# A two-layer hybrid decoder on one core: rests of the attention, pooling and gate weights by a negative copy and an adding transfer, with new priorities

## The chip, the core and the metric

The kernel runs on one core of a Trainium2 chip. The core has a matrix engine (TensorE, PE in the profile; its weight loads are PEld), VectorE (DVE), ScalarE (ACT), GpSimd (POOL) and SyncE (SP), which here only issues transfers. The engines run at the same time, each takes its instructions in order, and they wait for one another through semaphores. The metric is the device time of one execution in microseconds; less is better.

## What is computed

Two layers over 512 tokens of width 1024, then a last norm. Each layer has a sparse attention in which every query attends to its 128 best keys by an indexer's score, a gated linear attention, a pooling over trailing windows, and a convolutional feed-forward part. All in float32.

```python
def hybrid_layer(x, ...):
    h = rms_norm(x, norm1_g)
    qa, ka, va, qi, ki, wi, qb, kb, vb, rb, gl, uc = split_cols(h @ w_in)
    o_a = dsa_attention(rope(qa), rope(ka), va, rope(qi), rope(ki), wi)   # top-k keys, then softmax
    o_b = rms_norm(gla_chunked(qb, kb, vb, log_a(gl))) * silu(rb)
    o_c = multiscale_pool(uc, w_pool, pool_scale)
    x = x + concat(o_a, o_b, o_c) @ w_out
    return x + conv_glu_ffn(rms_norm(x, norm2_g), w_up, conv_w, conv_b, w_down)
```

## The kernel before

**Exact products of rounded halves.** The matrix engine takes float32 operands in a rounded format (F32R). So each operand is split into a rounded half and a rest, and `mm3` makes three matmuls of each product: rounded by rounded, rounded by rest, rest by rounded. For activations `split` and `split_scaled` do this. For weights `weights` (L567 on) does it. It cuts a matrix into chunks; of each chunk SyncE loads `raw` from memory (three buffers, `NRAW`), ACT copies it into the rounded half `hi`, and DVE subtracts the two into the rest `lo` (five buffers each, `NW`). A chunk of w_rb, w_uc, w_qk, w_gqk, w_qi, w_out and w_up is 128 partitions by 1024 values, as is one of w_v; those of w_tok and w_down are mostly smaller. `chunk` multiplies a 256-column matrix with the activations (output by columns), `tokens` makes the output by tokens (w_tok, 340 columns, and w_v, 512).

**The stages of a layer.** `layer` writes the work down in parts, by `nc.part`: start, qi, tok, ki (indexer), score1 to 3 and top1 to 3 (scores and the choice of keys of three query blocks, `choose`, sixteen rounds of maximum and replacement on DVE each), rb, gqk and gla (gates and the gated linear attention, whose chain runs over GpSimd, ACT and DVE), v, uc (pooling), qk (four chunks pairs of queries and keys; `rope` turns them with copies on SyncE's queue, `stacked` and `paired` lay their halves out with more copies), att0 to 3 (attention of each query block), out and ffn. In the times of the profile layer 0 lies at 0 to 632 us, its attention stage ending about 221; layer 1 follows, its attention stage ending about 821.

**What sets the order.** Nothing is issued as it is written. `Plan.take` records each instruction with a cost (`price`), its tiles and its dependences; `depend` adds an edge between two that touch the same data, with a delay for the signal from engine to engine (`delay`). `schedule` then orders all by a list plan in four passes: `forward` starts, on each engine that is free, the ready instruction of the highest priority for which buffers are free, and `backward` gives the priorities of the next pass. `HASTE` adds hand-set nanoseconds to the priority of a part, a part in a layer, or a part in a layer on an engine. A tile's buffer counts as free again some time after its last user ended: 2000 ns for SyncE's transfers, 200 ns for all others. `emit` issues the instructions of all engines in the order of the planned starts. On the chip each engine keeps that order, and only the semaphores decide when it goes on. Nearly all rows of the profile thus bear one line, L519, that of `emit`, and are told apart by their tiles.

The three lines at the heart of `weights`:

```python
nc.sync.dma_start(out=raw, in_=src[:, k0 * n:(k0 + kn) * n])
nc.scalar.activation(out=hf.bitcast(F32R), in_=raw, func=AF.Copy)
nc.vector.tensor_tensor(out=lf.bitcast(F32R), in0=raw, in1=hf, op=OP.subtract)
```

`price` has a branch for a transfer issued by GpSimd already (1050 ns); the kernel before has no such transfer.

Of the kernel before, what the change touches and what calls it, by code (L numbers as in the profile page):

```python
# [12 lines left out]
F32R = mybir.dt.float32r  # L13
I32 = mybir.dt.int32
U32 = mybir.dt.uint32
AF = mybir.ActivationFunctionType
OP = mybir.AluOpType
# [4 lines left out]
KC = D // P  # L22
# [30 lines left out]
def _constants():  # L53
# [26 lines left out]
    for c in range(2):  # L80
# [19 lines left out]
HASTE = {"top2": -52700, "gla": 1500, "score1": 43300, "att3": -100, "top3": -239100, "att0": 55600,  # L100
         "top1": -4600, "out": -7000, "rb": -6100, "rope": 68500, "ffn": 6800, "end": -97000, "end1": -7700,
# [31 lines left out]
         "gqk": 900}  # L133
WAVE = 1.2
SWITCH = 95.0
# [11 lines left out]
class Op:  # L147
    __slots__ = ("eng", "cost", "calls", "preds", "succs", "tiles", "func", "tags", "port", "shapes")

    def __init__(self, eng):  # L150
        self.eng, self.cost, self.calls = eng, 0.0, []
        self.preds, self.succs, self.tiles, self.func, self.tags = {}, {}, set(), None, set()
        self.port, self.shapes = False, []
# [12 lines left out]
class Plan:  # L166
# [50 lines left out]
    def depend(self, i, region, write):  # L217
        name = region[0]
        op = self.ops[i]
        old = self.access.setdefault(name, [])  # L220
        keep = []
        for j, r, w in old:
            if j != i and (write or w) and self.overlap(region, r):
                self.edge(j, i, self.delay(self.ops[j].eng, op.eng))
            covered = write and region[1] <= r[1] and r[2] <= region[2] and region[3] <= r[3] and r[4] <= region[4]
            if not covered or j == i:
                keep.append((j, r, w))
        keep.append((i, region, write))
        self.access[name] = keep
        op.tiles.add(name)  # L230

    def take(self, eng, fn, method, args, kw):
        out = kw.get("out", args[0] if args else None)
        ins = [x for k, x in list(enumerate(args)) + list(kw.items()) if hasattr(x, "tensor") and x is not out and k != "accum_out"]
        outs = [out] + ([kw["accum_out"]] if "accum_out" in kw else [])
        if self.open:
            op, i = self.ops[self.open[0]], self.open[0]
        else:
            op, i = Op(eng), len(self.ops)
# [6 lines left out]
        op.port = op.port or self.shared(eng, method, ins, out)  # L246
        if eng == "pe":
            rows, cols = (ins[0].shape[0], out.shape[0]) if method != "transpose" else (P, P)
            shape = tuple(32 if x <= 32 else 64 if x <= 64 else P for x in (rows, cols))
            if not op.shapes or op.shapes[-1] != shape:  # L250
                op.cost += SWITCH * bool(op.shapes)
                op.shapes.append(shape)
# [272 lines left out]
class Kern:  # L525
# [41 lines left out]
    def weights(self, src, k, n, whole=False):  # L567
        nc = self.pl
        out = []
        step = k if whole else min((k + 1) // 2, 1104 // n)  # L570
        for k0 in range(0, k, step):
# [6 lines left out]
            hf = hi.rearrange("p k n -> p (k n)")  # L578
# [3 lines left out]
            nc.vector.tensor_tensor(out=lf.bitcast(F32R), in0=raw, in1=hf, op=OP.subtract)  # L582
# [211 lines left out]
    def tokens(self, src, n):  # L794

        w = self.weights(src, KC, n)
# [347 lines left out]
    def layer(self, l):  # L1144
# [44 lines left out]
        w = self.weights(a["w_rb"][l], KC, 256)  # L1189
# [15 lines left out]
        w = self.weights(a["w_uc"][l], KC, 256)  # L1205
        for m in range(2):
            self.pool(l, m, self.chunk(w, m))
        for c in range(4):
            nc.part = "qk"
            w = self.weights(a["w_qk"][l, c], KC, 256)  # L1210
# [268 lines left out]
```

## Time and profile before

| | us |
|---|---|
| median of 3 runs (1227.28 to 1227.61) | 1227.35 |
| the profiled execution | 1230.25 |
| its span, first to last instruction | 1228.4 |
| PE busy | 1213.7 |
| DVE busy | 692.4 |
| ACT busy | 505.2 |
| GpSimd busy | 327.3 |

The span is what the trace covers; the profiled execution took 1.85 us more around it. A stretch is named by its microseconds from the start of the span. The granted clock is TensorE's, as a share of its full speed: 1.00 is the higher of its two levels, 2.4 GHz, 0.50 the lower, 1.2 GHz. Matmuls are pipelined, so that the busy spans of two of them overlap, and a busy PE need not be at its peak.

### The profile page before, as it was taken

To read this page: it belongs to the slowest core of one execution; us is meant where nothing else is said; L and a number is where in the kernel's file an instruction comes from. 1 tells how busy PE (TensorE), PEld (TensorE's weight loads), DVE (VectorE), ACT (ScalarE), POOL (GpSimd) and SP (SyncE) were. 2 spreads that over 40 slices of the span, in tenths; PEclk is the share of its full clock that TensorE was granted. 3 is DMA by queue.
4 is the path that set the end of the run, shared out by engine and by line. 5 is a ranking of instruction groups with operands and counts; after the bars stand their busy time and mean duration, and the time that the engine had idled before them with its cause. 6 is when DMAs were issued, how large, how long until landed. Compare 5 with 4: busy or idle time off the path is not lost.

```text
span 1228.4 us, 16614 instructions
## 1 busy us (share of the span) xinstructions
PE 1213.7 (99%) x6188; PEld 998.4 (81%) x6188; DVE 692.4 (56%) x1249; ACT 505.2 (41%) x819; POOL 327.3 (27%) x276
## 2 busy tenths in 40 slices
PE   9999999999999999999999999999999999999997
PEld 7878788888888888888897777888888888888887
DVE  7479986454553345444535999646355433454432
ACT  6562368443332134333425414864334322333331
POOL 1464351223221022221205623512122200222211
PEclk9999989999999999999999999999999999999998
DMA  8332464222223322224443135523222233332321
GB/s 272 112 95 76 129 158 138 69 87 85 87 71 105 125 94 99 90 78 126 147 137 92 52 109 153 152 86 103 69 95 89 89 95 114 103 103 92 95 72 69
DMA packets 49888, 129.38 MB, mean 105 GB/s; under 512 B 7488, under 2 KB 10320, under 8 KB 49808
## 3 DMA queue, kind: packets, MB, share of 16 engines
q1 hardware_dynamic: 49376, 128.05, 33.6%
q8 instruction: 49, 0.80, 0.3%
q10 hardware_dynamic: 432, 0.27, 0.1%
q14 instruction: 31, 0.25, 0.1%
HBM read 109.22 MB, written 4.26 MB: 92 GB/s over the span
## 4 chain that ended last, share of the span: by engine, by line
PE 87%; DVE 8%; issue 2%; POOL 2%; ACT 1%; DMA 0%; DVEq 0%; POOLq 0%; ACTq 0%
PE mm L519 78%; PE aux L519 9%; DVE score L519 2%; DVE m L519 2%; DVE lo L519 1%; DVE pl L519 1%; DVE qt L519 0%; POOL sl L519 0%; DVE att L519 0%; DMA raw<-in_w_out 0%; DVE q L519 0%; ACT L519 0%; POOL ke L519 0%; DVE k L519 0%; POOL ex L519 0%
## 5 line engine op out<-in xcount | busy, mean ns | idle before, releaser
L519 PE MATMUL mm<-xh,hi 128*128 128x512 f32 x960 | 379.8, 396 | 1.4 <-DVE q L519 1.2
L519 PE MATMUL mm<-xh,lo 128*128 128x512 f32 x960 | 374.7, 390 | 0.0
L519 PE MATMUL mm<-xl,hi 128*128 128x512 f32 x960 | 374.5, 390 | 0.0
L519 DVE TENSOR_TENSOR lo<-raw,hi 128x1024 fp32r<-128x1024 f32 (+3 forms) x210 | 244.6, 1173 | 181.4 <-ACT hi L519 178.6
L519 ACT ACTIVATE hi<-raw 128x1024 fp32r<-128x1024 f32 (+3 forms) x210 | 203.2, 975 | 341.4 <-PE mm L519 293.4
L519 PEld LDWEIGHTS mm<-xh,hi 128*128 128x128 f32 x960 | 180.6, 188 | 43.5 <-issue 6.6
L519 PEld LDWEIGHTS mm<-xh,lo 128*128 128x128 f32 x960 | 180.6, 188 | 38.4 <-DVE lo L519 0.4
L519 PEld LDWEIGHTS mm<-xl,hi 128*128 128x128 f32 x960 | 180.8, 188 | 36.5 <-issue 0.7
L519 PE MATMUL mm<-h,hi 128*128 128x512 f32 (+1 forms) x470 | 180.1, 383 | 0.0
L519 PE MATMUL mm<-h,lo 128*128 128x512 f32 (+1 forms) x470 | 178.3, 379 | 0.0
L519 PE MATMUL mm<-l,hi 128*128 128x512 f32 (+1 forms) x470 | 178.3, 379 | 0.0
L519 POOL TENSOR_TENSOR cv<-cv,rstd 128x512 f32<-128x512 f32 x44 | 57.9, 1318 | 299.9 <-ACT cv L519 292.0
L519 POOL TENSOR_TENSOR l<-cv,h 128x512 fp32r<-128x512 f32 x44 | 70.0, 1592 | 157.2 <-ACT h L519 149.0
L519 PEld LDWEIGHTS mm<-h,lo 128*128 128x128 f32 x470 | 88.4, 188 | 16.7
L519 PEld LDWEIGHTS mm<-h,hi 128*128 128x128 f32 x470 | 88.4, 188 | 16.5 <-issue 0.5
L519 PEld LDWEIGHTS mm<-l,hi 128*128 128x128 f32 x470 | 88.5, 188 | 15.8
L519 DVE SCALAR_TENSOR_TENSOR cv<-a,vec,cv 128x511 f32<-128x511 f32 (+1 forms) x88 | 71.8, 820 | 32.1 <-ACT cv L519 30.8
L519 ACT ACTIVATE cv<-a,vec 128x512 f32<-128x512 f32 x44 | 35.7, 814 | 125.2 <-DVE a L519 125.2
L519 DVE TENSOR_TENSOR a<-mm,rstd 128x512 f32<-128x512 f32 x44 | 30.3, 692 | 100.5 <-PE mm L519 100.4
L519 DVE TENSOR_TENSOR x<-x,mm 128x512 f32<-128x512 f32 (+1 forms) x50 | 33.1, 665 | 78.7 <-PE mm L519 75.3
L519 POOL TENSOR_TENSOR sq<-sq,sq 128x512 f32<-128x512 f32 x23 | 34.2, 1488 | 141.4 <-ACT sq L519 141.3
L519 ACT ACTIVATE cv<-cv 128x512 f32<-128x512 f32 x44 | 27.6, 632 | 61.2 <-DVE cv L519 61.2
(197 smaller groups left out, 1393.9 us busy)
## 6 DMA issues: line engine op xcount, KB each, us to landing
raw<-in_w_up SPq DMA_DIRECT2D x88, 512.0 KB, 3.8
raw<-in_w_down SPq DMA_DIRECT2D x32, 384.0 KB, 3.1
raw<-in_w_down SPq DMA_DIRECT2D x32, 320.0 KB, 2.9
raw<-in_w_qk SPq DMA_DIRECT2D x16, 512.0 KB, 3.8
raw<-in_w_out SPq DMA_DIRECT2D x16, 512.0 KB, 4.0
x<-in_x SPq DMA_DIRECT2D x16, 256.0 KB, 5.0
raw<-in_w_v SPq DMA_DIRECT2D x8, 512.0 KB, 4.1
raw<-in_w_rb SPq DMA_DIRECT2D x4, 512.0 KB, 4.2
```

The lines of the kernel that those rows point to most:

```text
L519: self.issued(i, fn(*args, **kw))
```

## The change

In `weights` a new argument `adds` selects how the rest is made. Where it is set, ACT makes a second copy, of `hi` times -1 into `lo`, and GpSimd's queue issues a transfer of `raw` into `lo` that adds to what is there. Where it is not set, DVE subtracts as before. It is set for w_rb, w_v (the only one with 512 columns), w_uc and w_qk, in both layers. The unused argument `whole` goes. The planner gets `LANDING`: a transfer issued by GpSimd delays all that depend on it by 3500 ns more. All of `HASTE` is replaced.

```diff
-HASTE = {"top2": -52700, "gla": 1500, "score1": 43300, "att3": -100, "top3": -239100, "att0": 55600,
...
-         "gqk": 900}
+HASTE = {"top2": -24800, "gla": 1500, "score1": 56200, "top3": -308500, "att0": 26200, "top1": -4500,
...
+         "qk.1": 3000, "att1.1.act": -4500, "qk": -100, "qi.1.pe": 300, "tok.0.pe": -400, "rb.0.act": 600}
 WAVE = 1.2
+LANDING = 3500.0
...
-    __slots__ = ("eng", "cost", "calls", "preds", "succs", "tiles", "func", "tags", "port", "shapes")
+    __slots__ = ("eng", "cost", "calls", "preds", "succs", "tiles", "func", "tags", "port", "shapes", "late")
...
-        self.port, self.shapes = False, []
+        self.port, self.shapes, self.late = False, [], 0.0
...
-                self.edge(j, i, self.delay(self.ops[j].eng, op.eng))
+                self.edge(j, i, self.delay(self.ops[j].eng, op.eng) + self.ops[j].late)
...
+        if eng == "pool" and method == "dma_start":
+            op.late = LANDING
...
-    def weights(self, src, k, n, whole=False):
+    def weights(self, src, k, n, adds=False):
...
-        step = k if whole else min((k + 1) // 2, 1104 // n)
+        step = min((k + 1) // 2, 1104 // n)
...
-            nc.vector.tensor_tensor(out=lf.bitcast(F32R), in0=raw, in1=hf, op=OP.subtract)
+            if adds:
+
+                nc.scalar.activation(out=lf.bitcast(F32R), in_=hf, func=AF.Copy, scale=-1.0)
+                nc.gpsimd.dma_start(out=lf, in_=raw, accum_op=OP.add)
+            else:
+                nc.vector.tensor_tensor(out=lf.bitcast(F32R), in0=raw, in1=hf, op=OP.subtract)
...
-        w = self.weights(src, KC, n)
+        w = self.weights(src, KC, n, n == 512)
...
-        w = self.weights(a["w_rb"][l], KC, 256)
+        w = self.weights(a["w_rb"][l], KC, 256, True)
...
-        w = self.weights(a["w_uc"][l], KC, 256)
+        w = self.weights(a["w_uc"][l], KC, 256, True)
...
-            w = self.weights(a["w_qk"][l, c], KC, 256)
+            w = self.weights(a["w_qk"][l, c], KC, 256, True)
```

## Rows read from the trace of the kernel before

**Rows 1.** Page, section 1: busy us (share of the span) and instructions of each engine.

```profile
PE 1213.7 (99%) x6188; PEld 998.4 (81%) x6188; DVE 692.4 (56%) x1249; ACT 505.2 (41%) x819; POOL 327.3 (27%) x276
```

**Rows 2.** Stretches: us, busy us (count) of PE, PEld, DVE, ACT, POOL; clock, DMA share, GB/s.

```profile
80.00:146.00 66.00, 65.79 (x320) 49.60 (x318) 65.62 (x169) 17.35 (x24) 26.59 (x28) 1.00 0.29 93
146.00:164.00 18.00, 17.55 (x153) 13.02 (x152) 17.74 (x44) 10.51 (x19) 7.26 (x6) 1.00 0.72 180
164.00:176.00 12.00, 11.80 (x63) 10.32 (x63) 8.01 (x29) 5.83 (x18) 7.53 (x6) 0.57 0.40 120
176.00:221.00 45.00, 45.00 (x405) 37.54 (x404) 28.19 (x99) 37.86 (x105) 11.47 (x9) 1.00 0.44 125
221.00:632.00 411.00, 411.00 (x1846) 342.20 (x1845) 192.53 (x220) 145.44 (x189) 87.89 (x59) 1.00 0.32 101
...
660.00:720.00 60.00, 58.16 (x294) 45.06 (x293) 55.70 (x134) 24.69 (x40) 32.12 (x41) 1.00 0.26 82
720.00:782.00 62.00, 59.72 (x369) 46.02 (x368) 59.45 (x151) 28.19 (x55) 20.00 (x16) 1.00 0.55 151
782.00:821.00 39.00, 38.68 (x379) 32.23 (x379) 19.05 (x75) 31.21 (x93) 10.63 (x8) 1.00 0.37 113
```

**Rows 3.** Waits of PE: engine waited for, us in total, times, longest us.

```profile
PE mm L519 <- DVE q L519: 1.2, 1, 1.2
PE aux L519 <- POOL ke L519: 1.2, 1, 1.2
...
PE aux L519 <- DVE att L519: 0.5, 1, 0.5
```

**Rows 4.** Timeline of PE, 719 to 722 us: start us, us, what, [idle before <-releaser].

```profile
719.71 0.39 PE L519 MATMUL mm<-xh,lo 128*128 128x512 f32 x1
721.32 0.47 PE L519 MATMUL mm<-xh,hi 128*128 128x512 f32 x1 [1.22 <-DVE q L519]
```

**Rows 5.** DMA issues: out<-in, engine, operation xcount, KB each, median us to landing.

```profile
raw<-in_w_qk SPq DMA_DIRECT2D x16, 512.0 KB, 3.8
...
raw<-in_w_v SPq DMA_DIRECT2D x8, 512.0 KB, 4.1
raw<-in_w_rb SPq DMA_DIRECT2D x4, 512.0 KB, 4.2
raw<-in_w_uc SPq DMA_DIRECT2D x4, 512.0 KB, 4.9
s0h<-sh SPq DMA_DIRECT2D x16, 128.0 KB, 2.4
```

**Rows 6.** Instructions by form: count | busy us, mean ns | idle before; last row 80 to 146 alone.

```profile
L519 DVE TENSOR_TENSOR lo<-raw,hi 128x1024 fp32r<-128x1024 f32 x140 | 178.2, 1277 | 110.5 <-ACT hi L519 107.8 <-PE aux L519 0.8
...
L519 ACT ACTIVATE hi<-raw 128x1024 fp32r<-128x1024 f32 x140 | 148.0, 1060 | 191.8 <-PE mm L519 160.8 <-issue 21.1 <-DMA raw<-in_w_rb 3.3
...
L519 DVE TENSOR_TENSOR lo<-raw,hi 128x1024 fp32r<-128x1024 f32 x11 | 13.3, 1213 | 0.0
```

**Rows 7.** Waits of all engines, columns as in rows 3: the rounding copy on ACT.

```profile
ACT hi L519 <- PE mm L519: 293.4, 128, 7.8
```

**Rows 8.** One issue on SyncE (timeline); one operation on GpSimd (instructions by form).

```profile
150.11 0.55 SPq L519 DMA_DIRECT2D rot<-q  x1
...
L519 POOL TENSOR_TENSOR sl<-q,sa 128x512 fp32r<-128x512 f32 x8 | 10.4, 1294 | 16.6 <-PE mm L519 8.1 <-ACT sa L519 6.1 <-ACT hi L519 2.2
```

**Rows 9.** Timelines of ACT and DVE in layer 1: a rounding copy, and its subtraction.

```profile
705.26 1.06 ACT L519 ACTIVATE hi<-raw 128x1024 fp32r<-128x1024 f32 x1 [3.96 <-PE mm L519]
...
711.26 2.33 DVE L519 TENSOR_TENSOR lo<-raw,hi 128x1024 fp32r<-128x1024 f32 x2
```

**Rows 10.** SyncE's queue: its longest wait; its timeline from 691 us.

```profile
SPq L519 <- DVE lo L519: 828.8, 181, 23.0
...
691.18 28.22 SPq L519 DMA_DIRECT2D raw<-in_w_qk  x5
721.25 0.52 SPq L519 DMA_DIRECT2D rot<-q  x1
```

More of the change, by code (lines that the diff above doesn't have):

```diff
@@ L99 @@
 PASSES = 4
-HASTE = {"top2": -52700, "gla": 1500, "score1": 43300, "att3": -100, "top3": -239100, "att0": 55600,
-         "top1": -4600, "out": -7000, "rb": -6100, "rope": 68500, "ffn": 6800, "end": -97000, "end1": -7700,
[31 rows of a table removed]
-         "gqk": 900}
+HASTE = {"top2": -24800, "gla": 1500, "score1": 56200, "top3": -308500, "att0": 26200, "top1": -4500,
[31 rows of a table added]
 WAVE = 1.2
+LANDING = 3500.0
 SWITCH = 95.0
```

61 rows, old and new, of the table HASTE are left out of this document.

## The prediction

> **What bounds the kernel now.** I read the busy shares first: TensorE (PE) is busy 1213.7 of 1228.4 us, VectorE (DVE) 692.4, ScalarE (ACT) 505.2, GpSimd (POOL) 327.3 [rows 1]. So PE's work is a floor that this change does not touch: it adds and removes no matmul. A gain can only come out of time in which PE waits or runs slowly. The cut into stages says where that is [rows 2]. In the feed-forward stretch 221 to 632 us PE is busy all of 411.00 us: nothing to win. The attention stages are different. In layer 0 PE lacks 0.21 us in 80 to 146, 0.45 in 146 to 164 and 0.20 in 164 to 176, together 0.9 us. In layer 1 it lacks 1.84, 2.28 and 0.32 us in the three stretches from 660 to 821, together 4.4 us. Beside that stands the granted clock: 0.57 on average over 164 to 176, so that PE is at the lower of its two levels (1.2 of 2.4 GHz) for most of it, and loses about (1 - 0.57) x 12 = 5.2 us of full-rate work there. The reader is to see in the same rows that DVE is the full engine: 65.62 of 66 us in 80 to 146, 55.70 of 60 and 59.45 of 62 in layer 1, while ACT is busy only 17.35 of 66 and GpSimd 26.59 of 66.
>
> Then I read who ended PE's waits [rows 3]: the longest is DVE's evacuation of q, 1.2 us, with another 0.5 behind DVE's work on att; GpSimd's ke holds PE for 1.2. The first one in order of time [rows 4]: matmuls follow one another about 0.23 us apart, each is shown 0.39 long, and the one at 719.71 is followed only at 721.32. The view reports 1.22 us of idle time where the gap in starts is 1.61, so it understates a wait by some 0.16 us, and waits shorter than that do not show at all.
>
> **Part 1: 32 subtractions leave DVE.** The pooling, gate and attention weights are the chunks of w_rb (4), w_v (8), w_uc (4) and w_qk (16), 32 in all [rows 5]. Each has one DVE subtraction of 128x1024. Its mean is 1.277 us over the whole run and 1.213 in 80 to 146 [rows 6], so DVE is relieved of 32 x 1.21 = 39 us, 19 per layer. In 80 to 146 us there are eleven of them; the last two are of w_out, whose loads come behind those of w_qk, and stay. So 9 x 1.21 = 11 of the 66 us go, and about as much from the full part of layer 1. This is no 39 us of time: PE is fed meanwhile from other chains. What DVE directly costs PE there is 1.2 + 0.5 = 1.7 us [rows 3]; I take all of it. Of the other 4.4 - 1.7 = 2.7 us of idle time in layer 1, GpSimd's ke among it, which itself comes out of the DVE chain of the gates, I take half, 1.4 us. What is late next is ACT: in 176 to 221 it is already busy 37.86 of 45 [rows 2], and nothing of the change relieves that stretch.
>
> **Part 2: 32 negative copies on ACT.** The nearest row is ACT's own rounding copy of the same shape, 1.060 us [rows 6], so 32 x 1.06 = 34 us, 17 per layer. Those of w_uc and w_qk land in 80 to 146 and 660 to 740, where ACT is idle more than half of the time [rows 2], those of w_rb and w_v ahead of it; that idle time hides them. If that cover is gone, as in 176 to 221, a copy costs its 1.06 us. Behind a copy on ACT's queue wait the next rounding copy and the gate chain's exponentials. The rounding copy usually waits for PE to give back a weight buffer anyway, 293.4 us in 128 waits [rows 7]. I take 0.
>
> **Part 3: 32 transfers on GpSimd's queue.** No row of before shows a transfer issued by GpSimd or one that adds, so both prices are bounded. The issue: below by SyncE's 0.55 us for one transfer, above by GpSimd's 1.294 for an ordinary operation on 128x512 [rows 8]; I take 1.1, nearer the second because it is that engine's own. That is 32 x 1.1 = 35 us on an engine that is 27% busy [rows 1]. The landing: below by the 2.4 us of a 128 KB copy inside the core, above by twice the 3.8 us of a 512 KB load, 7.6, since the sum must also read its destination [rows 5]; I take 5. The Trainium skill (DMA: Bandwidth & Descriptors, section on the anatomy of one DMA on the GpSimd path) fits such a transfer at about 2.0 us plus bytes over 436 GB/s, an estimate of 3.2 us for 512 KB; no run here shows one yet, the loads of that size took 3.8 from SyncE, and with 3.2 in place of 5 the sum below would be the same, as only the cover grows.
>
> A rest is thus ready 1.06 + 1.1 + 5 = 7.2 us (4.0 to 10.0) after its rounding copy, with no DVE queue in between. Today it is 1.2 us at best, but in the full stretch also more: the rounding copy of one w_qk chunk runs at 705.26 to 706.32 and the two subtractions next in line start at 711.26 [rows 9]. Does PE starve? A chunk feeds 24 matmuls x 0.23 = 5.5 us of PE, and five buffers leave four chunks, 22 us, of lead. 10.0 is below 22, so I cost the delay at nothing; that cover would be gone only if GpSimd held the issue back for more than 12 us.
>
> The transfer is a wait added to GpSimd's in-order queue: it waits for ACT's copy, and ke, kt, ex and osq of the gates are queued behind it. One hold of about the issue, 1.1 us, on something that PE waits for already (ke, 1.2 us), is likely in one or the other layer: I charge 1.5 us, with 0 to 4 as bounds. The raw buffer, too, is given back only at the landing: 7.2 - 1.2 = 6 us later than a prompt subtraction would.
>
> **Part 4: the new priorities.** All work is ordered anew, from a plan that now adds 3.5 us for the landing. The order of PE's work between 146 and 176 is what the clock hangs on: the fall at 164 comes behind 18 us in which weight loads were busy 13.02 us (72%) and PE sat between short attention matmuls; in 80 to 146 it was 49.60 of 66 (75%), in 720 to 782 46.02 of 62 (74%), and neither lost its clock [rows 2]. [...] With 11 us less DVE work ahead of this stretch, attention reaches PE earlier, while it still has weight chunks to mix in. I take the fall as gone, 5.2 us; a fall of the same length elsewhere would cost the same, and is the next case.
>
> **The sum.** 1.7 + 1.4 + 5.2 - 1.5 = 6.8 us. The profiled execution took 1230.25 us, 1.85 of it outside its span of 1228.4; it is 2.9 us above the median of the runs, 1227.35. Against itself: 1230.25 - 6.8 = 1223.45; against the median, which is what is asked: 1220.5.
>
> **Rivals.** (a) The low clock stays, or comes elsewhere; the waits go. 1227.35 - 1.6 = 1225.7, between 1223.5 and 1226.5. For it: the short attention matmuls of 146 to 164 stay as they are, and only their order changes. (b) More goes: all idle time of the two stages (0.9 + 4.4), the clock's 5.2 and as much again in waits too short to show: 1227.35 - 10.5 - 5 = 1212. For it: DVE is full for 130 us in both layers; against it: PE's idle time is small. (c) The relief is hidden anyway: PE's other chains end no earlier, and a stall moves from DVE to ACT. 1226.5 to 1228.5. (d) Slower: SyncE's in-order queue. The next load of raw weights waits for the buffer, today for DVE's subtraction (828.8 us in 181 waits), and then for the transfer's landing. Behind the loads on that queue stand the copies that turn and pair q and k: from 691.18 five loads of w_qk fill 28.22 us, and the first rot copy goes at 721.25 [rows 10]. The planner adds the 3.5 us to whoever reads the rest, but in its forward pass gives the raw buffer back 0.2 us after the issue, so its order of SyncE is too early by 3.3 us and more. It decides from the point where PE has used up its weight chunks before the pairs are there, about 146 and 740. Then 3 to 6 us per layer come on top, less the 3.1 of part 1: 1227.35 + 6 to 12 - 3 = 1230 to 1236. Against it: GpSimd's transfers themselves stand on another queue, and by 4 of 5 buffers the loads run early.
>
> **How the numbers follow.** Forecast 0.40 (1215 to 1223), (a) 0.22, (b) 0.10, (c) 0.08, (d) 0.20. About 0.2%, 2.5 us, is what a measurement of this kernel can tell from no change, so faster means under 1224.9: the forecast, (b) and half of (a), 0.61. Within: the other half of (a) and nearly all of (c), 0.18. Slower: (d) and a rest of (c), 0.21. The range leaves about one in ten out at either end: 1212 to 1232, from (b) to the lower half of (d).
>
> **What would show it.** Right: no subtraction rows of w_rb, w_v, w_uc and w_qk on DVE, ACT up by some 34 us, DVE down by some 39; DVE below full in 80 to 146; no wait of PE for DVE's q; the clock at 1.00 between 140 and 180. Landings of 4 to 7 us would confirm part 3. Wrong: PE waits that are ended by a transfer into lo, or SyncE waiting for such landings ahead of the rot copies, then (d); a low clock elsewhere, then (a); PE's idle time unchanged with ACT in DVE's place, then (c).

## The result, and the profile after

The changed kernel is slower. Its median is 1254.28 us (1252.02 to 1255.99, four runs) against 1227.48 us (1227.28 to 1228.71) of the kernel before, run beside it: a ratio of 1.0214 [1.0202, 1.0226]. That is 26.8 us more, where 6.8 less were forecast. The profiled execution took 1252.02 us, its span 1249.9, which is 21.5 us more than the span of before. Nearly all rows of after bear line L520, the one of `emit`.

The busy shares first, in the columns of [rows 1]:

```profile
PE 1214.7 (97%) x6188; PEld 999.0 (80%) x6188; DVE 675.8 (54%) x1217; ACT 533.7 (43%) x849; POOL 344.8 (28%) x308
```

PE's busy time is nearly as it was (1213.7 in [rows 1]), so it stands still for 1249.9 - 1214.7 = 35.2 us instead of 14.7. These 20.5 us of standing are all but one of the 21.5 us that the span grew by. The stretches say where; the columns are those of [rows 2]. The stretch 20 to 80 us of before was not among those rows, so it stands here, ahead of those of after:

```profile
20.00:80.00 60.00, 59.96 (x310) 50.71 (x310) 36.62 (x74) 35.27 (x54) 26.05 (x25) 1.00 0.44 134
```

```profile
20.00:80.00 60.00, 52.80 (x265) 44.25 (x265) 27.17 (x56) 36.50 (x48) 31.73 (x34) 0.94 0.79 202
80.00:146.00 66.00, 64.97 (x346) 49.48 (x345) 59.65 (x166) 29.40 (x43) 24.72 (x32) 1.00 0.50 123
146.00:164.00 18.00, 11.93 (x55) 9.35 (x54) 14.04 (x34) 5.29 (x8) 5.79 (x5) 0.81 0.54 155
164.00:176.00 12.00, 12.00 (x91) 9.53 (x91) 10.15 (x28) 5.43 (x14) 2.83 (x3) 1.00 0.76 180
...
221.00:632.00 411.00, 411.00 (x1894) 340.56 (x1893) 200.21 (x230) 152.13 (x209) 87.60 (x60) 1.00 0.31 98
...
660.00:720.00 60.00, 55.93 (x282) 43.08 (x281) 43.52 (x108) 36.31 (x55) 37.83 (x42) 0.97 0.54 127
720.00:782.00 62.00, 56.03 (x313) 44.00 (x311) 57.69 (x143) 22.65 (x31) 22.26 (x26) 1.00 0.73 178
```

PE lacks 7.2 us in 20 to 80 (0.04 before), 6.1 in 146 to 164 (0.45 before), 4.1 and 6.0 in layer 1 (1.8 and 2.3 before), and nothing in the feed-forward stretch. Read the column of the DMA engines beside it: 0.79 for 0.44, 0.50 for 0.29, 0.54 for 0.26, 0.73 for 0.55. In the feed-forward stretch, which has no new transfer, it is 0.31 for 0.32. Where PE stands and where the share grew do not match stretch by stretch: in 80 to 146 PE lacks only 1.0 us, and in 146 to 164 the share fell (0.54 for 0.72) while PE lacks 6.1. The last column but one of [rows 2] had the numbers of before, and the prediction did not use them.

The parts themselves, in the columns of [rows 6]: the subtractions left, the rounding copies, the negative copies on ACT, and the issues on GpSimd.

```profile
L520 DVE TENSOR_TENSOR lo<-raw,hi 128x1024 fp32r<-128x1024 f32 x108 | 141.2, 1312 | 102.1 <-ACT hi L520 97.2 <-PE aux L520 2.9
...
L520 ACT ACTIVATE hi<-raw 128x1024 fp32r<-128x1024 f32 x140 | 147.7, 1059 | 200.6 <-PE mm L520 186.1 <-DMA raw<-in_w_v 4.1 <-issue 3.2
...
L520 ACT ACTIVATE lo<-hi 128x1024 fp32r<-128x1024 f32 x32 | 33.5, 1053 | 0.6
...
L520 POOL DMA_DIRECT2D lo<-raw x32 | 28.9, 912 | 81.7 <-ACT lo L520 74.7 <-ACT relu L520 3.2 <-DVE small L520 2.0
```

DVE lost 32 subtractions, 178.2 - 141.2 = 37 us of them, though its busy time fell by 16.6 only, as others of its operations were stretched (the 56 products qt from 23.0 to 35.2 us). ACT gained 33.5 us of copies, and a transfer's issue holds GpSimd for 0.91 us. What PE and SyncE wait for, in the columns of [rows 3]:

```profile
PE mm L520 <- DVE q L520: 11.5, 4, 6.1
PE aux L520 <- DVE qt L520: 7.8, 3, 5.1
PE aux L520 <- DMA sa<-sl: 3.4, 1, 3.4
...
PE mm L520 <- DMA lo<-raw: 1.0, 1, 1.0
...
SPq L520 <- DVE lo L520: 722.4, 163, 21.0
SPq L520 <- DMA lo<-raw: 172.9, 29, 21.8
```

PE hardly waits for a rest itself (1.0 us). It waits for DVE's q and qt and for a copy inside the core, sa. The transfers of after, with the columns of [rows 5] and, in the first line, the new queue's packets, megabytes and share of the 16 DMA engines' time:

```profile
q0 software_dynamic: 4608, 16.78, 7.0%
...
lo<-raw POOLq DMA_DIRECT2D x32, 512.0 KB, 5.5
...
sa<-sl SPq DMA_DIRECT2D x12, 128.0 KB, 3.8
...
rot<-q SPq DMA_DIRECT2D x8, 64.0 KB, 4.2
rot<-k SPq DMA_DIRECT2D x8, 64.0 KB, 5.0
```

The same three small copies in the kernel before:

```profile
sa<-sl SPq DMA_DIRECT2D x12, 128.0 KB, 2.3
...
rot<-q SPq DMA_DIRECT2D x8, 64.0 KB, 2.0
rot<-k SPq DMA_DIRECT2D x8, 64.0 KB, 2.0
```

So copies that the change does not touch take 1.7 to 2.5 times as long to land. Two places show how that and GpSimd's queue reach PE. The first is PE's longest single wait, at 150 us. In order of time, the timelines of SyncE, DVE and PE (columns as in [rows 4]):

```profile
139.09 0.69 DVE L520 TENSOR_TENSOR k<-mm,rstd 128x512 f32<-128x512 f32 x1
...
140.58 3.14 SPq L520 DMA_DIRECT2D raw<-in_w_out  x2
143.77 1.56 SPq L520 DMA_DIRECT2D rot<-k  x1
...
149.96 0.01 DVE L520 LOAD_MASK_SELECT sh<-rot  x1 [6.14 <-DMA rot<-k]
...
156.07 0.67 DVE L520 TENSOR_TENSOR q<-mm,rstd 128x512 f32<-128x512 f32 x1
...
156.79 0.79 PE L520 MATMUL mm<-xh,hi 128*128 128x512 f32 x1 [6.07 <-DVE q L520]
```

What SyncE's queue waited for just then, 138 to 143.5 us (columns of [rows 3]):

```profile
SPq L520 <- DMA lo<-raw: 10.9, 2, 8.5
```

k is ready at 139.78, but rot<-k, its 64 KB copy, stands behind two loads of w_out on SyncE's queue, and these wait for the landings of two rests, the first 8.5 us and the second 2.4. So the copy is issued at 143.77, 4.0 us late, and it lands 6.0 us later, where such copies took 2.0 before (median): about half of its delay is the hold of the queue, half the longer landing. DVE, whose next instruction reads it, stands for 6.14 us until 149.96. In its order come the shuffle, seven maximum and replacement steps of the choice of keys, the sum rot and a subtraction, and only at 156.07 the evacuation of q for which PE stands 6.07 us. One late copy at the head of DVE's queue is paid in full by PE.

The second place is 64 to 75 us (timelines of DVE, GpSimd and PE):

```profile
64.76 10.15 DVE L520 TENSOR_TENSOR qt<-qb,ex 128x256 f32<-128x256 f32 x5 [4.72 <-ACT ex L520]
...
66.70 1.14 POOL L520 DMA_DIRECT2D lo<-raw  x1
67.31 1.82 POOL L520 TENSOR_TENSOR ke<-ke,gk 128x512 f32<-128x512 f32 x1
68.55 1.80 POOL L520 TENSOR_TENSOR l<-kg,h 64x512 fp32r<-64x512 f32 x1
69.78 3.00 POOL L520 TENSOR_TENSOR sl<-qi,sa 128x512 fp32r<-128x512 f32 x2
...
73.13 1.11 PE L520 MATMUL aux<-qt,kt 128*64 128x256 f32 x2 [5.09 <-DVE qt L520]
```

Five products qt on DVE took 10.15 us while GpSimd ran from operation to operation behind a transfer's issue; over the whole run of before, 56 of them took 23.0 us, 0.45 each. The second alone took 5.87 us, from 67.20 on; it is the one that PE's next matmuls read, and PE waited 5.09 us for it.

### The profile page after: what moved, and what is told of

The parts are those of the page before. It is cut to its first block, busy times and chain, and to the rows that moved or that the text cites. A ratio compares the mean times of both kernels' runs of the same rounds, so it can differ in the third digit from the quotient of the medians.

```text
span 1249.9 us, 16730 instructions
## 1 busy us (share of the span) xinstructions
PE 1214.7 (97%) x6188; PEld 999.0 (80%) x6188; DVE 675.8 (54%) x1217; ACT 533.7 (43%) x849; POOL 344.8 (28%) x308
## 3 DMA queue, kind: packets, MB, share of 16 engines
q0 software_dynamic: 4608, 16.78, 7.0%
## 4 chain that ended last, share of the span: by engine, by line
PE 85%; DVE 6%; DMA 3%; POOL 2%; issue 2%; ACT 1%; SPq 1%; DVEq 0%; POOLq 0%; ACTq 0%
PE mm L520 76%; PE aux L520 9%; DVE score L520 2%; DVE m L520 1%; DVE qt L520 1%; DMA s1l<-sl 1%; DMA rot<-k 1%; SPq L520 1%; POOL sl L520 1%; DMA lo<-raw 1%; DMA sa<-sl 0%; DMA raw<-in_w_v 0%; DMA q<-rot 0%; POOL rot L520 0%; DVE pl L520 0%
## 5 line engine op out<-in xcount | busy, mean ns | idle before, releaser
L520 PE MATMUL mm<-xh,hi 128*128 128x512 f32 x960 | 380.8, 397 | 11.5 <-DVE q L520 11.5
L520 PE MATMUL mm<-xh,lo 128*128 128x512 f32 x960 | 375.0, 391 | 1.0 <-DMA lo<-raw 1.0
L520 PE MATMUL mm<-xl,hi 128*128 128x512 f32 x960 | 374.8, 390 | 0.0
L520 ACT ACTIVATE hi<-raw 128x1024 fp32r<-128x1024 f32 (+3 forms) x210 | 203.0, 975 | 356.3 <-PE mm L520 324.3
L520 DVE TENSOR_TENSOR lo<-raw,hi 128x1024 fp32r<-128x1024 f32 (+3 forms) x178 | 207.6, 1174 | 171.2 <-ACT hi L520 166.2
L520 PEld LDWEIGHTS mm<-xh,hi 128*128 128x128 f32 x960 | 181.0, 189 | 53.2 <-DVE q L520 10.4
L520 PEld LDWEIGHTS mm<-xh,lo 128*128 128x128 f32 x960 | 180.8, 188 | 39.6 <-DMA lo<-raw 1.5
L520 PEld LDWEIGHTS mm<-xl,hi 128*128 128x128 f32 x960 | 180.9, 188 | 36.0 <-issue 0.5
L520 PE MATMUL mm<-h,hi 128*128 128x512 f32 (+1 forms) x470 | 179.5, 382 | 0.0
L520 PE MATMUL mm<-h,lo 128*128 128x512 f32 (+1 forms) x470 | 178.3, 379 | 0.0
L520 PE MATMUL mm<-l,hi 128*128 128x512 f32 (+1 forms) x470 | 178.2, 379 | 0.0
L520 POOL TENSOR_TENSOR cv<-cv,rstd 128x512 f32<-128x512 f32 x44 | 58.2, 1325 | 303.5 <-ACT cv L520 295.6
L520 POOL TENSOR_TENSOR l<-cv,h 128x512 fp32r<-128x512 f32 x44 | 69.5, 1581 | 153.7 <-ACT h L520 145.5
L520 PEld LDWEIGHTS mm<-h,lo 128*128 128x128 f32 x470 | 88.4, 188 | 16.7
L520 PEld LDWEIGHTS mm<-h,hi 128*128 128x128 f32 x470 | 88.4, 188 | 16.5 <-issue 0.3
L520 PEld LDWEIGHTS mm<-l,hi 128*128 128x128 f32 x470 | 88.4, 188 | 16.0
L520 DVE SCALAR_TENSOR_TENSOR cv<-a,vec,cv 128x511 f32<-128x511 f32 (+1 forms) x88 | 71.5, 817 | 34.2 <-ACT cv L520 32.9
L520 ACT ACTIVATE cv<-a,vec 128x512 f32<-128x512 f32 x44 | 35.7, 814 | 126.8 <-DVE a L520 126.8
L520 DVE TENSOR_TENSOR a<-mm,rstd 128x512 f32<-128x512 f32 x44 | 30.3, 691 | 98.5 <-PE mm L520 98.5
L520 DVE TENSOR_TENSOR x<-x,mm 128x512 f32<-128x512 f32 (+1 forms) x50 | 33.0, 665 | 75.7 <-PE mm L520 75.6
L520 POOL TENSOR_TENSOR sq<-sq,sq 128x512 f32<-128x512 f32 x23 | 33.9, 1473 | 138.9 <-ACT sq L520 138.9
L520 ACT ACTIVATE cv<-cv 128x512 f32<-128x512 f32 x44 | 27.6, 631 | 59.3 <-DVE cv L520 59.3
```

Source lines behind the costliest of these rows:

```text
L520: self.issued(i, fn(*args, **kw))
```

## The experiments

All ran three rounds beside the kernel before, whose median was between 1226.7 and 1228.0 us on each chip. Three questions: which part of the change costs the time, whether it is the transfers' bytes or their waits, and whether the plan could have avoided it.

**Priorities and transfers apart.** First the transfers with the priorities of before, and the new priorities without a transfer:

```diff
-HASTE = {"top2": -24800, "gla": 1500, "score1": 56200, "top3": -308500, "att0": 26200, "top1": -4500,
...
+HASTE = {"top2": -52700, "gla": 1500, "score1": 43300, "att3": -100, "top3": -239100, "att0": 55600,
...
```

This is the edit on the kernel after; on the kernel before it is the reverse.

> The transfers alone: the changed kernel with the priorities of before. Theory O (the operations are at fault: transfers that land late, and an issue on GpSimd's queue that lets GpSimd hold the port that DVE needs): 1240 to 1260 us, whatever the order. Theory P (the new priorities are at fault, the transfers are harmless): 1222 to 1230 us, about the kernel before.

Measured: 1264.4 us, ratio 1.0309 [1.0291, 1.0327].

> The priorities alone: the kernel before, DVE subtracting as ever, with the new priorities. Theory P: 1240 to 1255 us. Theory O: 1220 to 1235 us, since no transfer of GpSimd is left.

Measured: 1233.13 us, ratio 1.0054 [1.0039, 1.007]. The second kernel's profiled execution took 1236.48 us; its busy shares and the stretch in which its clock was low (the columns of [rows 1] and [rows 2]):

```profile
PE 1219.2 (99%) x6188; PEld 1001.1 (81%) x6188; DVE 702.2 (57%) x1249; ACT 508.0 (41%) x821; POOL 322.6 (26%) x276
```

```profile
157.50:174.60 17.10, 17.10 (x87) 13.65 (x85) 11.76 (x37) 2.98 (x10) 7.87 (x6) 0.50 0.63 159
```

PE's busy time is 5.5 us over that of before, and 17.1 us at half the clock lose 8.5 us of full-rate work, where before lost (1 - 0.57) x 12 = 5.2. So the transfers, with the copies and issues that belong to them, are the loss, 37 us with the old priorities. The new priorities cost 5.6 us by themselves and give back 1264.4 - 1254.3 = 10.1 beside the transfers. In this execution, which is 3.4 us above the kernel's median, they lengthen the very stretch of low clock that the prediction took as gone.

**The bytes taken out, the order held.** From here on most kernels keep the issue order of after on every engine, since the plan is made for the whole transfer and only the emitted instruction is exchanged. The first moves 16 of the 1024 columns:

```diff
                 nc.gpsimd.dma_start(out=lf, in_=raw, accum_op=OP.add)
+                nc.ops[-1].calls = [(self.nc.gpsimd.dma_start, (), dict(out=lf[:, 0:16], in_=raw[:, 0:16], accum_op=OP.add))]
```

> The order of the changed kernel is kept, and all 32 transfers are issued, but each moves 16 of the 1024 columns, so that 63/64 of the rests stay the negative copy. It separates two causes within theory O. If the bytes are at fault (512 KB of adding traffic before which other copies land late): 1228 to 1238 us. If the issue on GpSimd's queue is (DVE held from the port by back-to-back GpSimd work): 1245 to 1255 us. If half and half, about 1242: the first PE stall of 7.7 us at 65 us stays and those behind late copies go.

Measured: 1231.55 us (ten runs), ratio 1.0037 [1.0022, 1.0051]. The copy on ACT, the 32 issues on GpSimd, the wait of every reader for a landing and SyncE's wait for the raw buffer are all still there; 512 KB became 8. That alone takes 22.7 of the 26.8 us away. Its transfers, and the first two of PE's waits:

```profile
q0 software_dynamic: 4608, 0.26, 0.6%
...
lo<-raw POOLq DMA_DIRECT2D x32, 8.0 KB, 2.1
...
rot<-k SPq DMA_DIRECT2D x8, 64.0 KB, 2.8
```

```profile
PE mm L520 <- DVE q L520: 3.0, 2, 2.2
PE aux L520 <- DMA sa<-sl: 1.9, 2, 1.5
```

rot<-k lands in 2.8 us for 5.0, and PE's 11.5 us behind q are 3.0. SyncE still waits 136.1 us for landings, for 172.9. DVE's qt is held here too (five in 9.13 us at 63.19), yet all of PE's wait for qt is 1.0 us. GpSimd's issues by themselves are therefore not what makes that hold costly. What differs is the product that is held: here it is the fourth, for 5.95 us from 66.04 on, and PE reads it only at 72.10, behind matmuls of weights. The profiled execution was the fastest of the ten (1228.89 us), so its waits are on the low side.

The same cut with the priorities of before asks whether this depends on the order:

> The kernel with the priorities of before (that of 1264.4 us) and its order, with every transfer cut to 16 of the 1024 columns, so that the other columns of the 32 rests stay the negative of the rounded half. It asks what the transfers' bytes cost in another order, and what relief of DVE is worth beside the priorities of before. The cost goes with the bytes whatever the order: 1264.4 - 22.7, thus 1239 to 1245 us. Rival, the relief of DVE is worth something once the bytes are gone and the order is the one tuned for DVE: 1220 to 1230. Rival, this order is bad by itself (GpSimd's issues, ACT's copies), and the bytes add little: over 1250.

Measured: 1241.59 us, ratio 1.0116 [1.0099, 1.0133]. With what was run before, this makes a table of medians (us):

| | DVE subtracts | transfers of 8 KB | transfers of 512 KB |
|---|---|---|---|
| priorities of before | 1227.5 | 1241.6 | 1264.4 |
| new priorities | 1233.1 | 1231.6 | 1254.3 |

From the second column to the third the bytes cost 22.8 and 22.7 us, the same within the spread of the runs in two quite different orders. The way to PE is not the same in both. In the kernel of 1264.4 us (its line is L522) rot<-q and rot<-k land in 2.1 and 2.6 us, hardly later than in before, and PE's longest wait and its waits for the rests are:

```profile
PE aux L522 <- DMA sa<-sl: 7.5, 2, 7.4
...
PE mm L522 <- DMA lo<-raw: 5.1, 4, 3.2
```

Ahead of that copy into sa SyncE's queue waited 6.4 us for the landing of a rest; it was issued at 688.42, 5.1 us after its operand was ready, and landed 5.3 us later, where the median of before is 2.3. Again a held queue and a longer landing share one stall.

From the first column to the second, nearly free rests with 32 subtractions less on DVE change the time by +14.1 and -1.6 us, GpSimd's issues and ACT's copies included: a loss in one row, and nothing that the intervals of the two kernels (1.0039 to 1.007 and 1.0022 to 1.0051) tell from none in the other. In the row of the loss PE's longest wait is for qt (4.9 us, 5.9 in all). Subtractions left out with nothing in their place were not run, so what the relief of DVE is worth by itself is not shown.

**Half of the bytes, in three ways.** 512 of the 1024 columns in all 32 transfers; the 16 of w_qk whole and the others cut to 16 columns; and the reverse of that, which has `==` in the place of `!=`:

```diff
+                nc.ops[-1].calls = [(self.nc.gpsimd.dma_start, (), dict(out=lf[:, 0:512], in_=raw[:, 0:512], accum_op=OP.add))]
```

```diff
-            w = self.weights(a["w_qk"][l, c], KC, 256, True)
+            w = self.weights(a["w_qk"][l, c], KC, 256, 2)
...
+                if adds != 2:
+                    nc.ops[-1].calls = [(self.nc.gpsimd.dma_start, (), dict(out=lf[:, 0:16], in_=raw[:, 0:16], accum_op=OP.add))]
```

> The order of the changed kernel; each transfer moves 512 of the 1024 columns, the other half of each rest stays the negative copy. Whatever the bytes do, by traffic or by waits, this lies between the small transfers (1231.6 us) and the full ones (1254): if in proportion, 1243; if only landings beyond the planned 3.5 us hurt, about 1232, as 256 KB should land in some 3.7 us.

> The changed kernel's order, frozen; the transfers of w_qk (16) are whole, those of w_rb, w_v and w_uc (16) carry 16 of the 1024 columns, so that the other columns of those rests stay the negative of the rounded half. Half of the added bytes, all of them in the stages in which queries and keys are turned. Theory of shared transfers (each megabyte costs where copies that PE waits for are under way): these 16 lie beside the copies that turn and pair q and k and carry most of the 22.7 us between 8 KB and 512 KB: 1245 to 1252 us. Rival, the cost goes with the bytes wherever they are: 1243 us, as with half of the columns everywhere. Rival, GpSimd's and SyncE's waits behind the early weights (w_rb, w_uc) set it: 1233 to 1238.

> The changed kernel's order, frozen; the transfers of w_rb, w_v and w_uc (16) are whole, those of w_qk (16) carry 16 of the 1024 columns, so that the other columns of those rests stay the negative of the rounded half. The other half of the bytes. Theory of shared transfers at the copies of q and k: 1233 to 1238 us, PE's wait for qt at 65 us stays, its wait for q at 150 us goes. Rival, the cost goes with the bytes wherever they are: 1243 us. Rival, the early weights set it: 1245 to 1252.

Measured: 1243.02 us, 1.0116 [1.0096, 1.0135]; 1242.43, 1.0126 [1.0104, 1.0147]; 1241.07, 1.0129 [1.0093, 1.0165]. The three agree, and half of the bytes is half of the cost (11.5, 10.9 and 9.5 of 22.7 us), wherever they are: the rival, and not my theory that the transfers beside the copies of q and k carry most. Each half brings back its own stall, as PE's first wait shows, of the kernel with w_qk whole and then of the reverse:

```profile
PE mm L520 <- DVE q L520: 9.7, 4, 5.8
```

```profile
PE aux L520 <- DVE qt L520: 7.6, 2, 7.0
```

The wait for q (11.5 in after) belongs to the bytes of w_qk, the wait for qt (7.8) to those of the weights ahead of it.

**The adding taken out.** The same 512 KB as a plain copy, so that nothing of the destination is read:

```diff
-                nc.gpsimd.dma_start(out=lf, in_=raw, accum_op=OP.add)
+                nc.gpsimd.dma_start(out=lf, in_=raw)
```

> The order of the changed kernel; the 32 transfers copy the raw weights into the rest instead of adding, with the same bytes written and the destination not read, so that the rests hold the raw weights. If reading the destination and adding is what makes the landing long: it falls from 5.5 to about 4 us and the time to 1235 to 1245 us. If not: landing 5 to 5.5 us, time 1248 to 1256 us.

Measured: 1237.98 us, ratio 1.0077 [1.0054, 1.01].

```profile
q0 software_dynamic: 4608, 16.78, 3.5%
...
lo<-raw POOLq DMA_DIRECT2D x32, 512.0 KB, 3.4
```

The same 16.78 MB take half the DMA engines' time, and 16.3 us of the 22.7 are gone. One thing more changed: a plain copy's issue holds GpSimd for 0.58 us, one with adding for 0.91. From the shares: adding, 7.0% of 1249.9 us is 87 us of all 16 engines, 2.7 for each of the 32; plain, 3.5% of 1235.4 is 43 us, 1.35 each.

**The waiting taken out.** The transfers whole and adding, but into scratch buffers in device memory, so that nothing waits for them:

```diff
+        self.aside = [self.dr.tile([P, 1024], F32, ...) for i in range(4)]
...
+                nc.ops[-1].calls = [(self.nc.gpsimd.dma_start, (), dict(out=self.aside[self.nth % 4], in_=hf, accum_op=OP.add))]
```

> The order of the changed kernel; each of the 32 transfers moves its full 512 KB and adds, but from the rounded half into memory outside the core, so that neither the rest nor the raw buffer waits for its landing; the rests stay the negative copies. It separates traffic from waiting. If the traffic is at fault (other copies land late beside it): 1245 to 1255 us, with the turning copies rot<-q at 4 us and more as in the changed kernel. If the waits are (the rest and the raw buffer 5.5 us late): 1225 to 1233 us, as with the small transfers.

Measured: 1246.42 us, ratio 1.0147 [1.012, 1.0175]. With neither PE nor SyncE waiting for any of them, the transfers still cost 1246.4 - 1231.6 = 14.9 of the 22.7 us. They held the DMA engines somewhat longer than those of after (7.9% for 7.0), so this is a price for the traffic alone, not an exact share. rot<-k lands in 4.1 us here. By difference that leaves 7.9 us (1254.3 - 1246.4) for the waiting, an estimate.

**DVE put back in that order.** The negative copy is dropped, and the subtraction stands at the transfer's place in the issue order:

```diff
                 nc.scalar.activation(out=lf.bitcast(F32R), in_=hf, func=AF.Copy, scale=-1.0)
+                nc.ops[-1].calls = []
                 nc.gpsimd.dma_start(out=lf, in_=raw, accum_op=OP.add)
+                nc.ops[-1].calls = [(self.nc.vector.tensor_tensor, (), dict(out=lf.bitcast(F32R), in0=raw, in1=hf, op=OP.subtract))]
```

> The order of the changed kernel is kept instruction by instruction; only the negative copy and the transfer are replaced by DVE's subtraction, at the place of the transfer. Theory O: 1225 to 1238 us, most of the loss gone though DVE has 39 us more to do in an order that did not count with it. Theory P: 1245 to 1260 us.

Measured: 1252.83 us, ratio 1.0207 [1.019, 1.0224]. With no transfer at all, this order is as slow as after. Its stretch 80 to 146:

```profile
80.00:146.00 66.00, 57.50 (x296) 42.58 (x295) 65.62 (x163) 16.45 (x23) 16.32 (x22) 0.97 0.19 60
```

Here DVE is full (65.62 of 66) and PE starves (57.50). Against the kernel of 8 KB, relief of DVE is worth 21 us in an order that was made for it. The plans that know of the subtractions lose little or none of that (1233.1 and 1227.5 in the table): in them most of DVE's work on the rests is hidden.

**A plan that knows the landing.** `LANDING` at the measured size, and the raw buffer given back in the plan only after the landing:

```diff
-LANDING = 3500.0
+LANDING = 5500.0
...
-                    heapq.heappush(finish, (t + cost + (2000.0 if e == "dma" else 200.0), i))
+                    heapq.heappush(finish, (t + cost + (2000.0 if e == "dma" else 200.0 + op.late), i))
```

> The changed kernel with a plan that counts what was measured: 5500 ns instead of 3500 for the landing, and the raw buffer given back only after it. If the plan's false landing is the cause: 1225 to 1235 us. If the traffic itself delays copies that the plan cannot know of: 1240 to 1256 us.

Measured: 1250.09 us, ratio 1.0184 [1.0157, 1.0211]. That is 4.2 us less by the medians, with intervals that just overlap, so little or nothing. PE's first wait is now for the rests themselves:

```profile
PE mm L520 <- DMA lo<-raw: 6.2, 2, 4.9
```

Its copies of q and k land sooner, and PE waits only 0.8 us for q:

```profile
rot<-k SPq DMA_DIRECT2D x8, 64.0 KB, 3.0
```

The two wrong times in the plan are thus not the main cause of the loss, and neither is the stall at 150 us alone: another order stands elsewhere and is about as slow. The kernels with transfers in the order of after, by the time that their queue took of the DMA engines:

| kernel | MB added or copied | queue's share | landing, us | median, us |
|---|---|---|---|---|
| 8 KB each | 0.26 | 0.6% | 2.1 | 1231.6 |
| plain copy | 16.78 | 3.5% | 3.4 | 1238.0 |
| w_qk whole | 8.52 | 3.8% | 6.1 (whole) | 1242.4 |
| half of the columns | 8.39 | 3.8% | 3.6 | 1243.0 |
| others whole | 8.52 | 3.9% | 5.6 (whole) | 1241.1 |
| after | 16.78 | 7.0% | 5.5 | 1254.3 |
| traffic alone | 16.78 | 7.9% | 7.2 | 1246.4 |

Where the rests wait for the transfers, the time follows the share and not the landing of one transfer (3.6 and 6.1 us give the same time). The mean landing of all 32 would serve nearly as well, since the transfers cut to 8 KB land in 2.6 and 2.0 us beside the whole ones: 2.1, 3.4, 4.4, 3.6, 3.8 and 5.5 us in the order of the first six rows. So the table does not tell traffic from waiting; the last row does, for 14.9 of the 22.7 us. The plain copy lies some 3 to 5 us below the line of the others. No kernel of the study is faster than the one before.

## Why the prediction was wrong

**What bounds the kernel.** Right as far as it went: PE's busy time is a floor (1213.7 and 1214.7 us), the feed-forward stretches lose nothing, and all the change happens in PE's standing. Not read: the DMA engines' share in the same rows, 0.26 to 0.72 in the attention stages, as a resource that the change loads.

**Part 1, DVE relieved.** The 39 us measured 37. The gain of 3.1 us was not there: with the transfers nearly free the time is 4.1 us above before in the one order and 14.1 in the other. The argument took PE's 1.7 us of waits behind DVE and half of its other standing as going with the relief; the table's first two columns show no such gain in either order, with GpSimd's issues and ACT's copies in them. That the plan had hidden the subtractions already is the likely reason and fits the rows; it is argued and not shown.

**Part 2, the copies on ACT.** Size right, 33.5 us for 34. That they cost nothing was not tried alone; they are in the kernel of 8 KB with everything else that is not bytes.

**Part 3, the transfers.** This is the step that failed. Its two prices were good: 0.91 us for an issue (1.1 taken), 5.5 us for a landing (5 taken, bounds 2.4 and 7.6). The cover held in this order, as PE waits only 1.0 us for a rest; with the priorities of before it is 5.1. What the step did not have is a third price, what 32 transfers of 512 KB take from every other transfer. It charged 1.5 us, 0 to 4, for GpSimd's queue. The bytes alone measure 22.7 us, of which 14.9 stay with nobody waiting for the transfers. The waiting for landings, the raw buffer's later return among it, which the step named and charged nothing, is the other 7.9 or so, by difference. The sentence "I cost the delay at nothing" was right for the rest that is transferred and silent on rot, sa and the loads, which share the DMA engines with it. The Trainium skill says this (DMA: Bandwidth & Descriptors, section "Issuing engines are not separate DMA queues"): transfers of ScalarE, SyncE and GpSimd run on the same 16 DMA engines and interleave, whoever started them. The runs agree: rot<-k, issued by SyncE, lands after 2.0 us before and 5.0 us after, and transfers that nobody waits for cost 14.9 us. The fit of the Trainium skill that the prediction quoted (DMA: Bandwidth & Descriptors, section on the anatomy of one DMA on the GpSimd path) gives estimates of 3.2 us for 512 KB and 2.0 for 8 KB. A plain copy took 3.4 and the 8 KB sums 2.1, so it holds there, but the sums of 512 KB took 5.5.

**Part 4, priorities and clock.** The 5.2 us did not come, and most of them were probably not there to win. They were read in one execution, 2.9 us above the median, with a mean granted clock of 0.992. Of the 34 executions of the same kernel beside the experiments all but one had 0.994 to 0.998. Of the (1 - 0.992) x 1228.4 = 9.8 us of full-rate work that the profiled one lost to the clock, 5.2 are this stretch; without it its mean would be 0.996, like that of the others, an estimate. The sum took them from the median all the same. The stretch 164 to 176 is at 1.00, as forecast, but the clock is low elsewhere. One such stretch of after, in the columns of [rows 2]:

```profile
155.20:162.00 6.80, 5.21 (x12) 4.13 (x13) 6.80 (x16) 3.13 (x5) 1.30 (x2) 0.50 0.64 179
```

It lies behind PE's stand of 6.07 us, and others stand behind the waits for qt at 67 to 73 us (clock 0.94 on average in 20 to 80) and for sa at 674 (0.97 in 660 to 720). So in after it came with the stalls. The profiled execution of the kernel of 8 KB, without these long stands, is at full clock from 20 to 660 us, as in this stretch:

```profile
155.20:162.00 6.80, 6.80 (x78) 5.19 (x77) 6.72 (x20) 4.13 (x12) 1.04 (x1) 1.00 0.69 168
```

By themselves the new priorities did the opposite of what this part forecast: 17.1 us of low clock in one piece in the execution that was profiled, and 5.6 us more by the medians. That the order of PE's short and long matmuls sets the clock, as the part argued, no run here isolates.

**The rivals.** (d) had the right sign, and its sign was looked for in the right place: SyncE waits 172.9 us for landings, and rot<-k stands behind loads on its queue (143.77, behind two loads of w_out). At PE's longest stall its mechanism makes about half of the delay, the 4.0 us by which rot<-k is issued late. Over the whole it is the smaller part. The other 15 rot copies are issued at most 2.1 us after what they copy is ready, and their lateness is mainly the landing (median 5.0 us for 2.0 of rot<-k). With SyncE's waits left in (136.1 us) and the bytes taken out, 22.7 us go; with nobody waiting for the transfers, about 7.9; with its plan mended, 4.2 by the medians. Its price, 6 to 12 us less 3.1, was right in size for that waiting and had no term for what the traffic costs by itself. (c)'s core, that the relief is hidden anyway, fits the table, and all that the transfers cost comes on top.

**The range** ended at 1232 us, since no term of it could grow with bytes. Worked out from rows of before, such a term was possible as a warning, if not as a price: 32 sums of 512 KB move 16.8 MB and read as much of their destination, in two stages of some 200 us each whose DMA engines were 26 to 72% busy already [rows 2].

**What stays open.** How the 22.7 us split between late loads, late small copies and DVE's order behind them was not measured one by one; only the stalls for q and qt were tied to the weights that cause them, and they belong to this order. The hold of DVE's qt costs PE 5 us beside full transfers because the second product is held, and 1 us beside those of 8 KB, where it is the fourth; what shifted the two engines against each other was not tried. The 4.1 us by which the 8 KB kernel lies above before are GpSimd's issues, ACT's copies, waits of 2 us and the priorities together, less what the relief of DVE gives.

## What to carry to other kernels

Before work goes from an engine to a transfer, read the DMA share of the stages that it goes to and price the transfer as occupation of the DMA engines, not as a latency: an adding copy occupied them 2.7 us for 512 KB here, twice a plain one, and the copies at PE's longest stalls landed 5.3 and 6.0 us after their issue, where the medians of such copies were 2.3 and 2.0 before. Ask too what else stands on the queue that waits for the landing. A full engine is no gain by itself where a planner has already put its work under the matrix engine's; what counts is PE's waits behind it (1.7 us here). To tell the two apart on the chip, hold the issue order and shrink the transfer's bytes, then keep the bytes and let nobody wait.

## What the runs showed of the hardware

- A sum of 512 KB inside the core, issued by GpSimd, landed in 5.5 us, a plain copy of the same size in 3.4, one of half the size with adding in 3.6 and of 8 KB in 2.1. The issue held GpSimd about 0.91 us, that of the plain copy 0.58.
- 64 KB copies between partitions, issued by SyncE, landed in 2.0 us in the kernel before and in 4.2 and 5.0 us beside the sums. With 8 KB transfers in the same order they took 2.3 and 2.8, and beside full sums with the priorities of before 2.1 and 2.6: the medians depend on the order.
- The cost of the bytes was the same within the spread (22.7 and 22.8 us) in two different issue orders, and half for half of the bytes, in either half of the weights.
- Two-operand products on DVE stood still while GpSimd ran operation after operation: five qt in 10.15 us, one of them 5.87. The Trainium skill (SBUF — State Buffer, section "Who interferes with whom") states that DVE shares a pair of ports with GpSimd under an exclusive lock, and that a DVE instruction with two inputs in the core's memory contends with a GpSimd instruction that reads that memory; these rows agree. The 56 qt took 23.0 us in before, 32.1 with 8 KB transfers and 35.2 in after. The longest qt was 1.1 us in before and 1.5 in the order of after with DVE's subtractions, 5.9 with transfers of 8 KB and of 512 KB alike. An issue of GpSimd is not shown to be needed for a hold: another two-input operation of before, st, took 4.3 us.
